# A streaming-encoder layer: elementwise work taken off GpSimd, the first stage rewritten, two inner orders changed

## The chip, the cores and the metric

The kernel runs on one core of a Trainium2 chip. A core has TensorE (PE in the profile, with its weight loads as PEld), VectorE (DVE), ScalarE (ACT), GpSimd (POOL) and SyncE (SP), which here only issues DMAs. The engines run side by side, each its own queue in order, and wait for each other by semaphores. The metric is the device time of one launch in microseconds (us). Before the change the median of three runs is 1245.73 us (1245.38 to 1246.48).

## The reference, cut to what matters

One layer on 1024 tokens with 1024 channels, all float32:

```python
h = rmsnorm(x, norm1_g)                       # per token: x * rsqrt(mean(x^2)+eps) * g
xa, ya, sq, sk, sv, dq, dk, dv = split(h @ w_in)
out_a = rg_lru(causal_dwconv(xa)) * gelu(ya)  # gates by two block matrices, then a scan over time
out_b = stick_breaking(sq, sk, sv)            # 4 heads of 64, strictly causal
out_c = diff_attention(dq, dk, dv)            # softmax(q1 k1) - lam * softmax(q2 k2), 4 heads,
                                              # then an rmsnorm over each head's 64 values (sub-norm)
x = x + concat(out_a, out_b, out_c) @ w_out
u = causal_dwconv(rmsnorm(x, norm2_g) @ w_ff_up)
x = x + (silu(gate(u)) * val(u)) @ w_ff_down
return rmsnorm(x, final_g)
```

## The kernel before, in words

**Split products.** Every large product is made from three products of half operands: an operand is written as `hi` (a cast to a shorter format, fp32r) and `lo` (the rest, operand minus `hi`), and hi·hi, hi·lo and lo·hi are added in PSUM. So each weight tile of 128 x 1024 values costs one cast and one subtraction on an elementwise engine before PE can use it (`split_to`, lines 135 to 152). In the profile a weight is `raw_dk`, `hi_dk`, `lo_dk` and so on, and its product is `pj_dk`. Weight tile number i has its cast on DVE for i below `VECTOR_HI` and its subtraction on GpSimd for i from 4 to 19 (`POOL_LO`), else on DVE.

**First stage** (lines 599 to 625). The 1024 tokens come in eight tiles `x_0` to `x_7`. For each tile a step `n` does the norm: ACT squares and sums the row (`junk`), takes a square root (`ry`); DVE refines 1/sqrt in five small instructions on 128x1 (`rv`, `ry`, `rq`); GpSimd multiplies the row by the gain `gb` (`xg`). The norm factor goes in for tiles 0 to 3 as a diagonal matrix `dg` that PE multiplies with while it transposes, for tiles 4 to 6 by a DVE multiplication, for tile 7 by ACT. A step `t` transposes the tile on PE (`tp`, eight blocks of 128x128), ACT casts the result to `hTh` and DVE subtracts to `hTl`. A step `s` splits weight tiles. The table `START` is the order in which ACT and DVE get these steps; it is kept as written. On PE the order is set by a list scheduler when the program is built, and then stands.

**First projections.** `start_pair` runs `dk` and `dq` on tokens 0 to 511 (24 products each) and then on tokens 512 to 1023; the third weight, `dv`, follows after both. Between the two halves stand `setup_lru` (some thirty DVE instructions on 128x4, `wl`) and `setup_tab` (the distance table `tab`).

**Attention.** A loop over 64 pairs (head, block of 128 queries): scores on PE (`sd`, `ss`), exponentials on ACT, differences or scans on DVE (`e`, `gam`, `bet`). GpSimd masks `gam` and `bet` by a select. The other 17 projections are cut in pieces (`filler`) and handed to PE between these steps. In `weighted` the probabilities of a pair of blocks are transposed chunk by chunk on PE (`pt`), copied by ACT (`ph`), and multiplied with the values (`av`) in `gather`, one chunk behind. `sub_norm` runs once for each pair of heads, one step per loop turn: squares and sums (`sq`, `ssq`), 1/sqrt by small DVE instructions (`bv`, `by`, `bq`), then for each half a broadcast on DVE (`bc`), its transposition on PE (`rb`) and the final product on DVE.

**Rest.** The output projection with the second norm (in its last group, for tokens 512 and up, two sums of the Strassen-like up-projection run on GpSimd: `t4_sum`, `t4_parts`), the gated MLP up-projection, and the down-projection, in which `right_half` multiplies by the final gain on GpSimd.

Instructions emitted through the recording helper all show line L62.

Of the kernel before, what the change touches and what calls it, by code (L numbers as in the profile page):

```python
# [46 lines left out]
def hybrid_trunk(ctx: ExitStack, tc: tile.TileContext, x, norm1_g, w_in, conv_a_w, conv_a_b,  # L47
# [66 lines left out]
    def add_cols(name, w2d, c0):  # L114
        job_no[name] = len(jobs)
        jobs.append((name, w2d[:, c0:c0 + P].rearrange("(k p) c -> p k c", p=P), True, None))
# [52 lines left out]
    for c in range(4):  # L169
# [3 lines left out]
             "xa2", "sk1", "sq1", "sv1", "ya2", "xa3", "ya3"]  # L173
    for nm in first + later:
        add_cols(nm, w_in[0], FT[nm])
# [80 lines left out]
    def transpose_split(xg, dg, hh, hl, t):  # L256
        q = (t % 4) * P
        for j in range(2):
            ps = bank_t(f"tp_{t}_{j}").rearrange("p (a b) -> p a b", a=4)
            for k in range(4):  # L260
                blk = xg[:, (4 * j + k) * P:(4 * j + k + 1) * P]
                if dg is None:
                    T.transpose(out=ps[:, k, :], in_=blk, identity=ident)
                else:
                    T.matmul(ps[:, k, :], lhsT=blk, rhs=dg, start=True, stop=True)
# [22 lines left out]
    wm = bank_t("warm")  # L288
# [54 lines left out]
    def setup_lru():  # L343
# [68 lines left out]
    chores = []  # L412
# [131 lines left out]
    def project(name, early=False):  # L544
        hi, lo = weights(name)
        if early:
            both = two_banks(f"pj_{name}")
        for h in range(2):
            if early:
                ps = both[:, h * HALF:(h + 1) * HALF]  # L550
            else:
                ps = bank_t(f"pj_{name}_{h}")
# [46 lines left out]
    with tc.manual_schedule(engines={nc.scalar.engine, nc.vector.engine}):  # L599
        dg1 = {}  # L600
        for step in START:
            t = int(step[1])
            if step[0] == "n":
                vy = rsqrt_start(xts[t], junk, 1.0 / D)
                xg1[t] = at4(f"xg1_{t}")[:, 0:D]
                cut = D // 4 if t == 0 else 0
                if cut:
                    V.tensor_tensor(xg1[t][:, 0:cut], xts[t][:, 0:cut], gb1[:, 0:cut], ALU.mult)
                G.tensor_tensor(xg1[t][:, cut:D], xts[t][:, cut:D], gb1[:, cut:D], ALU.mult)
                rr = rsqrt_end(*vy)  # L610
                dg1[t] = None
                if SCALE_1[t] == "D":
                    dg1[t] = diagonal(rr, c2(f"dg1_{t}", F32)[:, 0:P])
                elif SCALE_1[t] == "A":
                    A.activation(xg1[t], xg1[t], AF.Identity, scale=rr)
                else:
# [85 lines left out]
    def weighted(ptiles, vt, hh, j, put, name, nh):  # L702
        av = ps1.tile([P, P], F32, tag="av", name=f"av_{name}")
        held = None
# [9 lines left out]
        for c in range(j + 1):  # L714
# [16 lines left out]
        gather(*held)  # L731
# [16 lines left out]
    def sub_norm(p, o):  # L748
        ss = bank_t(f"ssq_{p}")
        for c in range(2):  # L750
            cs = slice(c * HALF, (c + 1) * HALF)
            sq = c2(f"sq_{p}_{c}", F32)
            A.activation(sq, o[:, cs], AF.Square)
            for b in range(4):
                q = 4 * c + b
                T.matmul(ss[:, 2 * q:2 * q + 2], lhsT=sq[:, b * P:(b + 1) * P], rhs=bones,
                         start=True, stop=True)
# [8 lines left out]
        yield  # L766
        for c in range(2):
            cs = slice(c * HALF, (c + 1) * HALF)
            bc_ = c2(f"bc_{p}_{c}", F32)
            V.tensor_copy(bc_.rearrange("p (q h d) -> p q h d", q=4, h=2),  # L770
                          y[:, 8 * c:8 * c + 8].rearrange("p (q h) -> p q h", h=2).unsqueeze(3)
                          .broadcast_to([P, 4, 2, 64]))
            ps = bank_t(f"rb_{p}_{c}")
            for b in range(4):
                T.transpose(out=ps[:, b * P:(b + 1) * P], in_=bc_[:, b * P:(b + 1) * P], identity=ident)
# [568 lines left out]
    for grp in range(4):  # L1344
        toks = (2 * grp, 2 * grp + 1)
        pss = {t: two_banks(f"oc_{t}") for t in toks}
        for ki, kt in enumerate(STREAM + (KEEP if grp == 0 else [])):
# [25 lines left out]
            if grp == 3:  # L1373
                if ki == 1:
# [3 lines left out]
                    t4_sum(4, G)  # L1378
                if ki == 2:
# [4 lines left out]
                    t4_sum(5, G)  # L1384
# [202 lines left out]
    def right_half(t):  # L1587
# [3 lines left out]
        G.tensor_scalar(ssr[t], ssr[t], 1.0 / D, EPS, ALU.mult, ALU.add)  # L1591
        G.tensor_tensor(o, acc[t][:, H1], gfin[:, H1], ALU.mult)
# [113 lines left out]
```

## Time and profile before

| | |
|---|---|
| median of three runs | 1245.73 us |
| profiled execution, its time | 1245.19 us |
| its span, first to last instruction | 1243.5 us |
| PE busy | 1181.2 us (95%) |
| DVE busy | 930.8 us (75%) |
| ACT busy | 638.5 us (51%) |
| GpSimd busy | 137.8 us (11%) |
| mean granted TensorE clock | 0.981 of full |

How to read it: PE is the engine that is nearly always busy, so the time is PE's work, plus PE's idle time, plus what PE loses in stretches in which it was granted less than its full clock. What the other engines do matters where PE waits for them. The rows further down are taken from four views: the page, the waits of PE, the instructions in order of time, and busy time by stretches of the span.

### The profile page before, as it was taken

Reading aid. Unit: us, or ns where it says so; the run is one execution under the profiler, and the core shown is the slowest. Engines: PE = TensorE matmul, PEld = TensorE weight load, DVE = VectorE, ACT = ScalarE, POOL = GpSimd, SP = SyncE. Lnnn points to the kernel's source line nnn. Section 1 sums busy time; section 2 is a strip of 40 time slices with the busy share of each in tenths; the row PEclk is TensorE's granted clock in tenths of the full one; section 3 lists DMA queues with packets and bytes.
Section 4 is the critical chain, followed back from the end, with each engine's and each line's share of the span. In section 5 each row is a group of like instructions: output and inputs, shape, how many; then the busy total and the mean of one; then the engine's idle time right before and its main releaser. Section 6 shows DMA issues by size and latency. Waiting matters only on the chain.

```text
span 1243.5 us, 15374 instructions
## 1 busy us (share of the span) xinstructions
PE 1181.2 (95%) x5731; PEld 918.4 (74%) x5731; DVE 930.8 (75%) x1361; ACT 638.5 (51%) x1046; POOL 137.8 (11%) x187
## 2 busy tenths in 40 slices
PE   5899999999899998998899999999999999999997
PEld 4777676666676666776578888888888888888886
DVE  7746557655763688677999988898888968856776
ACT  3424476637444765543555545545555554433455
POOL 6002011012333230003000000000000000000210
PEclk7989998999899999999999999999999999999999
DMA  5111011201122354831233233332323269832223
GB/s 188 52 34 37 18 35 54 51 22 39 45 52 79 110 169 154 306 102 34 71 100 110 94 110 95 100 111 94 101 90 114 94 207 315 302 107 93 93 77 136
DMA packets 121116, 130.42 MB, mean 105 GB/s; under 512 B 6401, under 2 KB 85713, under 8 KB 121041
## 3 DMA queue, kind: packets, MB, share of 16 engines
q1 hardware_dynamic: 120529, 129.17, 32.5%
q8 instruction: 45, 0.74, 0.2%
q0 software_dynamic: 512, 0.26, 0.1%
q14 instruction: 30, 0.25, 0.1%
HBM read 96.64 MB, written 32.77 MB: 104 GB/s over the span
## 4 chain that ended last, share of the span: by engine, by line
PE 58%; DVE 8%; ACT 4%; issue 3%; DMA 1%; POOL 1%; DVEq 0%; ACTq 0%; POOLq 0%
PE ad L62 18%; PE b L62 10%; PE u L62 9%; PE v L62 7%; PE e L62 4%; PE oc L62 3%; PE av_s L62 1%; PE pj_ya L62 1%; DMA raw_wo<-in_w_out_dram 1%; PE pj_sq L62 1%; PE pj_sv L62 1%; PE pt_s L62 1%; DVE gam L62 1%; PE ss L62 1%; DVE t L62 1%
## 5 line engine op out<-in xcount | busy, mean ns | idle before, releaser
L62 ACT COPY u<-ad 128x512 f32<-128x512 f32 x44 | 25.7, 585 | 116.6 <-PE ad L62 116.6
L62 DVE CUSTOM_DVE_ANT_0 e<-sd,tab 128x128 f32<-128x128 f32 (+7 forms) x64 | 46.3, 754 | 48.1 <-PE sd L62 48.0
L62 ACT ACTIVATE e<-e,mn 128x128 f32<-128x128 f32 (+7 forms) x64 | 49.6, 776 | 51.5 <-DVE mn L62 51.5
L62 DVE TENSOR_TENSOR al<-ar,ah 128x1024 fp32r<-128x1024 f32 x35 | 44.5, 1270 | 42.1 <-ACT ah L62 39.9
L62 ACT CAST ah<-ar 128x1024 fp32r<-128x1024 f32 x35 | 36.6, 1045 | 67.2 <-issue 31.8
L62 PE MATMUL ad<-h2h,xh 128*128 128x512 f32 x176 | 69.8, 397 | 1.1 <-ACT oc L62 1.1
L1591 POOL TENSOR_SCALAR sr<-sr 128x1 f32<-128x1 f32 x8 | 3.5, 432 | 606.8 <-ACT dw L62 606.8
L62 PE MATMUL ad<-h2h,xl 128*128 128x512 f32 x176 | 69.5, 395 | 0.0
L62 PE MATMUL ad<-h2l,xh 128*128 128x512 f32 x176 | 69.5, 395 | 0.0
L62 PE MATMUL e<-T,w 128*128 128x512 f32 x264 | 65.5, 396 | 0.8 <-ACT T L62 0.5
L62 PE MATMUL u<-bh,ah 128*128 128x512 f32 x160 | 62.7, 392 | 0.2 <-DVE cg L62 0.2
L62 PE MATMUL u<-bl,ah 128*128 128x512 f32 x160 | 62.6, 391 | 0.0
L62 PE MATMUL u<-bh,al 128*128 128x512 f32 x160 | 62.5, 391 | 0.0
L62 DVE SCALAR_TENSOR_TENSOR va<-cv,fcol,va 128x1023 f32<-128x1023 f32 (+1 forms) x44 | 56.5, 1284 | 7.0 <-ACT va L62 6.2
L62 DVE TENSOR_TENSOR_SCAN gam<-gam 128x128 f32<-128x128 f32 (+7 forms) x32 | 44.2, 1383 | 22.9 <-POOL gam L679 22.9
L62 PE MATMUL b<-T,yh 128*128 128x512 f32 x176 | 56.6, 403 | 4.2 <-DVE t L62 2.5
L62 DVE SCALAR_TENSOR_TENSOR ga<-cg,fcol,ga 128x1023 f32<-128x1023 f32 (+1 forms) x44 | 56.5, 1283 | 4.8 <-ACT ga L62 3.8
L62 PEld LDWEIGHTS e<-T,w 128*128 128x128 f32 x264 | 49.5, 188 | 13.4 <-ACT T L62 1.0
L62 PE MATMUL b<-B,zh 128*128 128x512 f32 x176 | 55.4, 396 | 1.6 <-DVE cv L62 1.6
L62 PE MATMUL ad<-T,zh 128*128 128x512 f32 x176 | 55.5, 396 | 0.5 <-ACT u L62 0.5
L62 PE MATMUL ad<-T,yh 128*128 128x512 f32 x176 | 55.3, 395 | 0.0
L62 PE MATMUL oc<-hi_wo,mx 128*128 128x512 f32 x160 | 52.7, 399 | 0.4 <-ACT oc L62 0.4
(398 smaller groups left out, 3364.8 us busy)
## 6 DMA issues: line engine op xcount, KB each, us to landing
qd<-g SPq DMA_DIRECT2D x77, 256.0 KB, 2.0
ar<-qd SPq DMA_DIRECT2D x35, 512.0 KB, 4.0
raw_wo<-in_w_out_dram SPq DMA_DIRECT2D x23, 512.0 KB, 3.8
rg<-in_w_ff_up_dram SPq DMA_DIRECT2D x22, 512.0 KB, 5.1
rv<-in_w_ff_up_dram SPq DMA_DIRECT2D x22, 512.0 KB, 4.0
dw<-in_w_ff_down_dram SPq DMA_DIRECT2D x20, 512.0 KB, 6.7
mx<-m SPq DMA_DIRECT2D x24, 256.0 KB, 5.2
x<-in_x_dram SPq DMA_DIRECT2D x8, 512.0 KB, 7.8
```

What stands on the lines that cost most here:

```text
L62: ins = emit(*args, **kw)
L1591: G.tensor_scalar(ssr[t], ssr[t], 1.0 / D, EPS, ALU.mult, ALU.add)
```

## The change

- **First stage.** The norm step is now one DVE instruction over the whole row, `xg = x * r * g`; no diagonal matrices, no GpSimd, no ACT scaling. All eight transpositions use the identity. Four small products of a zero matrix (`warm`) follow the transpositions of tiles 0 to 2. The order table is new: each transposition comes one norm step later, and the first weight is split before the fourth tile's transposition.
- **First weights.** The casts of the first three weights move to ACT. The third weight `dv` gets its own buffer (`third`). `start_three` runs `dk`, `dq` and `dv` on tokens 0 to 511 and then all three on tokens 512 to 1023. `setup` comes between the halves, `setup_tab` later, `setup_lru` becomes a chore taken in four pieces during the attention.
- **GpSimd.** All weight subtractions, `t4_sum`, `t4_parts` and `right_half` go to DVE. GpSimd keeps the fills, the selects, the index table and its 16 small DMAs.
- **Gathers.** `gather` runs for two chunks together, up to two chunks behind.
- **Sub-norm.** Its steps are cut finer: squares; sums; 1/sqrt; both broadcasts; then each half's transposition and product.

```diff
-START = "n0 n1 n2 t0 n3 t1 s1 t2 n4 t3 n5 n6 t4 n7 s2 t5 t6 t7".split()
-SCALE_1 = "DDDDVVVA"
-POOL_LO = range(4, 20)
-VECTOR_HI = 23
+WARM_T = 4
+START = "n0 n1 t0 n2 t1 n3 t2 s1 t3 n4 s2 n5 t4 n6 t5 n7 s3 t6 t7".split()
+VECTOR_HI = range(3, 23)
...
-            if i < VECTOR_HI:
+            if i in VECTOR_HI:
                 V.tensor_copy(hi, raw)
             else:
                 A.copy(hi, raw)
-            (G if i in POOL_LO else V).tensor_tensor(lo, raw, hi, ALU.subtract)
+            V.tensor_tensor(lo, raw, hi, ALU.subtract)
...
+    def start_three(names, between):
+        w = [parts.pop(nm) for nm in names]
+        ps = [two_banks(f"pj_{nm}") for nm in names[:2]]
         for h in range(2):
+            for i, nm in enumerate(names):
+                bank = ps[i][:, h * HALF:(h + 1) * HALF] if i < 2 else bank_t(f"pj_{nm}_{h}")
                 for k in range(KT):
+                    mm3(bank, *w[i], k, h, slice(0, HALF))
+                consumers[nm](h, bank)
+                for fn in between.get((h, i), ()):
                     fn()
...
-                cut = D // 4 if t == 0 else 0
-                if cut:
-                    V.tensor_tensor(xg1[t][:, 0:cut], xts[t][:, 0:cut], gb1[:, 0:cut], ALU.mult)
-                G.tensor_tensor(xg1[t][:, cut:D], xts[t][:, cut:D], gb1[:, cut:D], ALU.mult)
-                rr = rsqrt_end(*vy)
-                dg1[t] = None
-                if SCALE_1[t] == "D":
-                    dg1[t] = diagonal(rr, c2(f"dg1_{t}", F32)[:, 0:P])
-                elif SCALE_1[t] == "A":
-                    A.activation(xg1[t], xg1[t], AF.Identity, scale=rr)
-                else:
-                    V.tensor_scalar(xg1[t], xg1[t], rr, None, ALU.mult)
+                V.scalar_tensor_tensor(xg1[t], xts[t], rsqrt_end(*vy), gb1, ALU.mult, ALU.mult)
             elif step[0] == "t":
-                transpose_split(xg1[t], dg1[t], hTh[t // 4], hTl[t // 4], t)
+                transpose_split(xg1[t], hTh[t // 4], hTl[t // 4], t)
+                if t < 3:
+                    for _ in range(WARM_T):
+                        T.matmul(wm[:, 0:P], lhsT=zero, rhs=xg1[t][:, 0:P], start=True, stop=True)
...
-        setup()
-        start_pair(first[0], first[1], [setup_lru, setup_tab])
-        for _ in project(first[2], early=True):
-            pass
+        load_to(4)
+        start_three(first, {(0, 2): [setup], (1, 0): [lambda: ahead(first[2], 0)], (1, 1): [setup_tab]})
...
-            if held is not None:
-                gather(*held)
-            held = (c, pt)
+            held.append((c, pt))
+            if len(held) == 3:
+                gather(*held.pop(0))
+                gather(*held.pop(0))
...
     def sub_norm(p, o):
+        sqs = [c2(f"sq_{p}_{c}", F32) for c in range(2)]
+        for c in range(2):
+            A.activation(sqs[c], o[:, c * HALF:(c + 1) * HALF], AF.Square)
+        yield
         ss = bank_t(f"ssq_{p}")
...
+        bcs = [c2(f"bc_{p}_{c}", F32) for c in range(2)]
+        for c in range(2):
+            V.tensor_copy(bcs[c].rearrange("p (q h d) -> p q h d", q=4, h=2),
+                          y[:, 8 * c:8 * c + 8].rearrange("p (q h) -> p q h", h=2).unsqueeze(3)
+                          .broadcast_to([P, 4, 2, 64]))
+        yield
...
-                    t4_sum(4, G)
+                    t4_sum(4, V)
...
-                    t4_parts(4, G)
+                    t4_parts(4, V)
                     prep_x(1)
                     prep_x(0)
-                    t4_parts(5, G)
+                    t4_parts(5, V)
...
-        G.tensor_scalar(ssr[t], ssr[t], 1.0 / D, EPS, ALU.mult, ALU.add)
-        G.tensor_tensor(o, acc[t][:, H1], gfin[:, H1], ALU.mult)
+        V.tensor_scalar(ssr[t], ssr[t], 1.0 / D, EPS, ALU.mult, ALU.add)
+        V.tensor_tensor(o, acc[t][:, H1], gfin[:, H1], ALU.mult)
```

How the order moves is shown at three places. First DVE's queue in the opening, from the second norm step to the first tile's `hTl`. Before:

```order
L62 TENSOR_SCALAR dg_1_180<-ident,ry 128x128
L62 TENSOR_SCALAR rv<-ss 128x1
L62 RECIPROCAL ry<-ry 128x1
L62 SCALAR_TENSOR_TENSOR rq<-ry,rv 128x1
L62 TENSOR_SCALAR rq<-rq 128x1
L62 TENSOR_TENSOR ry<-ry,rq 128x1
L62 TENSOR_SCALAR dg_2_195<-ident,ry 128x128
L62 TENSOR_TENSOR hTl_145<-tp_0_197,hTh_143 128x4x128
L62 TENSOR_TENSOR hTl_145<-tp_1_204,hTh_143 128x4x128
```

The same place of DVE's queue in the changed kernel:

```order
L61 SCALAR_TENSOR_TENSOR xg_1_170<-x_1_125,ry,gb_121 128x1024
L61 TENSOR_TENSOR hTl_145<-tp_0_177,hTh_143 128x4x128
L61 TENSOR_TENSOR hTl_145<-tp_1_184,hTh_143 128x4x128
L61 TENSOR_SCALAR rv<-ss 128x1
L61 RECIPROCAL ry<-ry 128x1
L61 SCALAR_TENSOR_TENSOR rq<-ry,rv 128x1
L61 TENSOR_SCALAR rq<-rq 128x1
L61 TENSOR_TENSOR ry<-ry,rq 128x1
L61 SCALAR_TENSOR_TENSOR xg_2_201<-x_2_127,ry,gb_121 128x1024
```

The first tile's subtraction moved ahead of the third norm, and the wide multiplication stands in DVE's queue.

Second PE's queue at the seams between the first products: end of `dq` on the first tokens, start of `dk` on the last tokens, and the seam from `dq` to `dv`. Before:

```order
L62 MATMUL pj_dq_413<-hTh_143,lo_dq_343 128x512
L62 MATMUL pj_dk_412<-hTh_144,hi_dk_240 128x512
...
L62 MATMUL pj_dq_413<-hTh_144,lo_dq_343 128x512
L62 MATMUL pj_dv_559<-hTh_143,hi_dv_467 128x512
L62 MATMUL pj_dv_559<-hTl_145,hi_dv_467 128x512
```

PE's queue at the same seams in the changed kernel:

```order
L61 MATMUL pj_dq_395<-hTh_143,lo_dq_289 128x512
L61 MATMUL tp_1_385<-ident,xg_7_352 128x128 x4
L61 MATMUL pj_dv_0_449<-hTh_143,third 128x512
L61 MATMUL pj_dv_0_449<-hTl_145,third 128x512
...
L61 MATMUL pj_dv_0_449<-hTh_143,third 128x512
L61 MATMUL pj_dk_394<-hTh_144,hi_dk_257 128x512
```

`dv` on the first tokens moved ahead of `dk` on the last tokens, and the last transposition stands just before it.

Third PE's queue at the sub-norm of the first head pair, where `rb` transposes the first broadcast `bc_0`. Before:

```order
L62 MATMUL sd_6_0_1914<-qk_d_715 128x384
L62 MATMUL sd_6_1_1915<-qk_d_715 128x384
L62 MATMUL rb_0_1869<-ident,bc_0_1867 128x128 x4
L62 MATMUL pt_d_1_1_1878<-ident,e_3_0_1725 128x128
L62 MATMUL pt_d_1_1_1878<-ident,e_2_0_1651 128x128
```

PE's queue around the same transposition in the changed kernel:

```order
L61 MATMUL pt_d_2_0_1981<-ident,e_5_0_1844 128x128
L61 MATMUL sd_7_0_2001<-qk_d_700 128x512
L61 MATMUL sd_7_1_2002<-qk_d_700 128x512
L61 MATMUL rb_0_2018<-ident,bc_0_1918 128x128 x4
L61 MATMUL pj_sq_0_2024<-hTh_143,hi_sq_1822 128x512
```

`rb_0` moved back by more than one loop turn: from behind the scores of block 6 to behind those of block 7.

## Rows read from the trace of the kernel before

**Rows 1.** The page: busy time, share of the span and instructions of each engine.

```profile
PE 1181.2 (95%) x5731; PEld 918.4 (74%) x5731; DVE 930.8 (75%) x1361; ACT 638.5 (51%) x1046; POOL 137.8 (11%) x187
```

**Rows 2.** By stretch: us, length, each engine's busy us, granted clock, DMA share, GB/s.

```profile
0.00:31.00 31.00, 15.71 (x84) 14.77 (x84) 23.33 (x33) 11.95 (x24) 20.69 (x25) 0.78 0.55 189
...
124.00:400.00 276.00, 263.26 (x1542) 189.22 (x1542) 167.33 (x308) 151.82 (x288) 58.33 (x85) 0.96 0.15 43
```

**Rows 3.** PE's waits: what waited for what: us in total, times, longest us.

```profile
PE tp L62 <- DVE rv L62: 7.4, 1, 7.4
PE rb L62 <- DVE bc L62: 5.9, 2, 3.9
PE pj_dv L62 <- DVE qk_d L62: 4.0, 1, 4.0
...
PE av_d L62 <- ACT ph_d L62: 2.1, 1, 2.1
PE av_s L62 <- ACT ph_s L62: 1.8, 1, 1.8
```

**Rows 4.** DVE in order of time: start us, us, operation; 20 to 62 us.

```profile
20.53 2.12 DVE L62 SCALAR_TENSOR_TENSOR rq<-ry,rv 128x1 f32<-128x1 f32 x1
...
23.27 1.28 DVE L62 TENSOR_TENSOR hTl<-tp,hTh 128x512 fp32r<-128x512 f32 x2
24.47 0.14 DVE L62 TENSOR_SCALAR rv<-ss 128x1 f32<-128x1 f32 x1
...
24.72 0.22 DVE L62 SCALAR_TENSOR_TENSOR rq<-ry,rv 128x1 f32<-128x1 f32 x1
...
25.36 0.29 DVE L62 TENSOR_SCALAR dg<-ident,ry 128x128 f32<-128x128 f32 x1
...
29.16 1.23 DVE L62 TENSOR_TENSOR lo_dk<-raw_dk,hi_dk 128x1024 fp32r<-128x1024 f32 x1
...
61.65 1.23 DVE L62 SCALAR_TENSOR_TENSOR tab<-tab 128x1024 f32<-128x1024 f32 x1
```

**Rows 5.** GpSimd in order of time, first stage.

```profile
6.73 15.90 POOL L609 TENSOR_TENSOR xg<-x,gb 128x768 f32<-128x768 f32 x7 [4.50 <-DMA gb<-in_norm_g_dram]
```

**Rows 6.** By stretch, at 18 to 22 us, columns as in the second group.

```profile
18.00:22.00 4.00, 1.23 (x8) 0.97 (x8) 3.93 (x4) 1.46 (x4) 4.00 (x2) 0.93 0.12 28
```

**Rows 7.** ACT in order of time, the second tile's norm.

```profile
7.89 1.06 ACT L62 ACTIVATE junk<-x 128x1024 f32<-128x1024 f32 x1 [1.91 <-DMA x<-in_x_dram]
...
9.07 0.29 ACT L62 ACTIVATE ry<-ss,eps 128x1 f32<-128x1 f32 x1
```

**Rows 8.** PE in order of time, first projections, with idle time ahead in brackets.

```profile
33.37 1.16 PE L62 MATMUL tp<-ident,xg 128*128 128x128 f32 x8 [0.92 <-DVE xg L62]
34.28 0.48 PE L62 MATMUL pj_dk<-hTl,hi_dk 128*128 128x512 f32 x1
...
63.53 0.79 PE L62 MATMUL pj_dv<-hTh,hi_dv 128*128 128x512 f32 x1 [4.00 <-DVE qk_d L62]
...
79.80 0.48 PE L62 MATMUL pj_dk<-hTh,hi_dk 128*128 128x512 f32 x1
```

**Rows 9.** By stretch, three stretches at a low granted clock.

```profile
63.50:69.00 5.50, 5.46 (x13) 4.30 (x14) 2.46 (x3) 0.00 (x0) 0.00 (x0) 0.50 0.31 88
...
204.00:212.00 8.00, 8.00 (x27) 6.73 (x27) 6.62 (x17) 1.89 (x5) 0.00 (x0) 0.50 0.20 59
...
332.00:336.00 4.00, 4.00 (x13) 3.12 (x12) 1.69 (x3) 1.37 (x2) 0.00 (x0) 0.57 0.00 0
```

**Rows 10.** Groups by line: DVE at 60 to 485 us, and GpSimd.

```profile
L62 DVE SCALAR_TENSOR_TENSOR s<-s,nlam,s 128x1 f32<-128x1 f32 x32 | 14.4, 450 | 1.0
...
L150 POOL TENSOR_TENSOR lo_ya<-raw_ya,hi_ya 128x1024 fp32r<-128x1024 f32 x4 | 9.6, 2392 | 50.5 <-DVE hi_ya L62 40.1 <-PE pj_ya L62 7.8 <-PE pt_s L62 2.6
...
L1592 POOL TENSOR_TENSOR dw<-acc03b,gfin 128x512 f32<-128x512 f32 x4 | 7.4, 1844 | 0.3
```

**Rows 11.** DVE in order of time, end of the output projection.

```profile
570.71 2.31 DVE L62 TENSOR_TENSOR xl<-rg,xh 128x1024 fp32r<-128x1024 f32 x1
```

More of the change, by code (lines that the diff above doesn't have):

```diff
@@ L112, in hybrid_trunk, with add_cols @@
     direct = set()
-    def add_cols(name, w2d, c0):
+    def add_cols(name, w2d, c0, dst=None):
         job_no[name] = len(jobs)
-        jobs.append((name, w2d[:, c0:c0 + P].rearrange("(k p) c -> p k c", p=P), True, None))
+        jobs.append((name, w2d[:, c0:c0 + P].rearrange("(k p) c -> p k c", p=P), True, dst))
     def add_row(name, w2d, k, dst=None):
@@ L173, in hybrid_trunk, with third @@
              "xa2", "sk1", "sq1", "sv1", "ya2", "xa3", "ya3"]
+    def third():
+        w = b16("third", (P, 2, 8, P))
+        return w[:, 0], w[:, 1]
     for nm in first + later:
-        add_cols(nm, w_in[0], FT[nm])
+        add_cols(nm, w_in[0], FT[nm], third if nm == first[2] else None)
     STREAM = [6, 0, 1, 7, 4]
@@ L253, in rsqrt_bits, with transpose_split @@
         return y
-    def transpose_split(xg, dg, hh, hl, t):
+    def transpose_split(xg, hh, hl, t):
         q = (t % 4) * P
@@ L260, in transpose_split @@
             for k in range(4):
-                blk = xg[:, (4 * j + k) * P:(4 * j + k + 1) * P]
-                if dg is None:
-                    T.transpose(out=ps[:, k, :], in_=blk, identity=ident)
-                else:
-                    T.matmul(ps[:, k, :], lhsT=blk, rhs=dg, start=True, stop=True)
+                T.transpose(out=ps[:, k, :], in_=xg[:, (4 * j + k) * P:(4 * j + k + 1) * P], identity=ident)
             h = hh[:, 4 * j:4 * j + 4, q:q + P]
@@ L285, in c2 @@
         return att.tile([P, HALF], dt, tag="c2", name=name, bufs=6)
-    wm = bank_t("warm")
+    wm = ps1.tile([P, P], F32, tag="av", name="warm")
     for _ in range(WARM):
@@ L358, in setup_lru @@
             V.tensor_scalar(po, po, 1.0 / n, None, ALU.add)
+            if n in (9, 3):
+                yield
         V.tensor_tensor(po, po, z, ALU.mult)
@@ L411, in hybrid_trunk @@
     lru = {}
-    chores = []
+    chores = [setup_lru()]
     last_scan = []
@@ L541, in hybrid_trunk, with project @@
         consumers[f"ya{c}"] = branch_y(c)
-    def project(name, early=False):
+    def project(name):
         hi, lo = weights(name)
-        if early:
-            both = two_banks(f"pj_{name}")
         for h in range(2):
[L549 to L552, printed above, removed]
+            ps = bank_t(f"pj_{name}_{h}")
             for k in range(KT):
@@ L599, in hybrid_trunk @@
     with tc.manual_schedule(engines={nc.scalar.engine, nc.vector.engine}):
-        dg1 = {}
         for step in START:
@@ L703, in weighted @@
         av = ps1.tile([P, P], F32, tag="av", name=f"av_{name}")
-        held = None
+        held = []
         def gather(c, pt):
@@ L725, in weighted @@
                 V.tensor_copy(pt[:, b0 * P:], tp[:, b0 * P:])
-            if held is not None:
-                gather(*held)
-            held = (c, pt)
+            held.append((c, pt))
+            if len(held) == 3:
+                gather(*held.pop(0))
+                gather(*held.pop(0))
             yield
         yield
-        gather(*held)
+        for h_ in held:
+            gather(*h_)
         put(av)
@@ L748, in sub_norm @@
     def sub_norm(p, o):
+        sqs = [c2(f"sq_{p}_{c}", F32) for c in range(2)]
+        for c in range(2):
+            A.activation(sqs[c], o[:, c * HALF:(c + 1) * HALF], AF.Square)
+        yield
         ss = bank_t(f"ssq_{p}")
[L750 to L757, printed above, removed]
+        for q in range(8):
+            T.matmul(ss[:, 2 * q:2 * q + 2], lhsT=sqs[q // 4][:, (q % 4) * P:(q % 4 + 1) * P], rhs=bones,
+                     start=True, stop=True)
         c1 = sums[p]
@@ L766, in sub_norm @@
         yield
+        bcs = [c2(f"bc_{p}_{c}", F32) for c in range(2)]
[3 more added lines that the diff above has]
+                          .broadcast_to([P, 4, 2, 64]))
+        yield
         for c in range(2):
             cs = slice(c * HALF, (c + 1) * HALF)
[L769 to L772, printed above, removed]
             ps = bank_t(f"rb_{p}_{c}")
             for b in range(4):
-                T.transpose(out=ps[:, b * P:(b + 1) * P], in_=bc_[:, b * P:(b + 1) * P], identity=ident)
+                T.transpose(out=ps[:, b * P:(b + 1) * P], in_=bcs[c][:, b * P:(b + 1) * P], identity=ident)
             V.scalar_tensor_tensor(o[:, cs], o[:, cs], gsub, ps, ALU.mult, ALU.mult)
@@ L968, in norm2_t @@
             B["h"], B["l"] = b16("h2h"), b16("h2l")
-        transpose_split(hns.pop(t), None, B["h"], B["l"], t)
+        transpose_split(hns.pop(t), B["h"], B["l"], t)
     def banks_of(t):
@@ L1383, in hybrid_trunk @@
                     last_tokens(5)
-                    t4_sum(5, G)
+                    t4_sum(5, V)
                 if ki == 4:
-                    t4_parts(4, G)
+                    t4_parts(4, V)
                     prep_x(1)
                     prep_x(0)
-                    t4_parts(5, G)
+                    t4_parts(5, V)
         if grp == 0:
```

13 lines of the change are left out of this document (removed).

## The prediction

> **What bounds the kernel now.** I read the page's busy times first. PE works 95% of the span [rows 1], so the time is PE's work plus what PE idles or loses to a low clock. Then the stretches: in the first 31 us PE is busy for 15.7 us at a mean granted clock of 0.78, and from 124 to 400 us it idles 276.0 - 263.3 = 12.7 us at 0.96, while DVE is busy 167 of 276 us, 61% [rows 2]. Third, PE's waits name the places: the first transpositions, the sub-norm's `rb`, the start of `dv`, and the value products `av` that wait for their copied chunks [rows 3]. Only these places can give time back; a DVE or GpSimd instruction elsewhere costs nothing.
>
> The opening is slow for a reason that the order of instructions shows. An instruction on 128x1 values (`rq`) takes 2.12 us at 20.5 us and 0.22 us four microseconds later [rows 4]. In between GpSimd ends its seven gain products, 15.9 us in one go from 6.7 us on [rows 5]. It isn't the DMA traffic: at 18 to 22 us the DMA engines are busy for 0.12 of the time, and DVE is still full [rows 6]. So DVE's small instructions wait for GpSimd's, and every norm step pays several of these 2 us.
>
> **First stage.** The change empties GpSimd there and prices everything on DVE by undisturbed rows. A norm chain takes 25.36 - 24.47 = 0.9 us [rows 4]. The wide `xg`, two SBUF operands and a scalar on 128x1024, isn't in the trace; the nearest row is `tab`, the same operation and size, 1.23 us, 1.2 back to back. A tile's two `hTl` are 24.47 - 23.27 = 1.2, a weight's `lo` 1.2 [rows 4]. The second tile's square root ends at 9.07 + 0.29 = 9.4 us, and the tile itself had landed at 7.9 [rows 7]. From there DVE has, before PE can run the first product without a stop: three norm steps (3 x 2.1), the `hTl` of three tiles (3 x 1.2), `lo_dk` (1.2) and half the fourth tile's `hTl` (0.6). That is 11.7, so PE starts at 9.4 + 11.7 = 21.1 us, where it now starts at 34.3 [rows 8]. ACT's casts and squares run beside it.
>
> From there to the first product of the next weight (`dk1`) PE now takes 79.8 - 34.3 = 45.5 us [rows 8]. Of this go the wait of 4.0 before `dv` [rows 3, 8], since thirty `wl` instructions and the table no longer stand in front of `qk_d`, and half of the 5.5 us at clock 0.50 behind that wait, 2.7 [rows 9]. One tile's transpositions come in, 1.2 [rows 8]. That leaves 40.0, and `dk1` starts at 61.1: 18.7 us earlier.
>
> Does DVE keep up with three first halves? After 21.1 it has half an `hTl`, four norm steps, four `hTl` and two `lo`: 0.6 + 8.4 + 4.8 + 2.4 = 16.2, done at 37.3. PE's 72 products take about 0.21 us each at full clock (13 take 5.5 us at half [rows 9]), 15.1, and four tiles' transpositions 4.6, so it needs the second tokens at 40.8. The margin is 3.5 us; at `dv`, whose `lo` comes at about 34.5, it is about 1 us. SP now puts three weight loads ahead of the nine small parameter loads; the third waits for a buffer until `dv` is split, so these come 20 us later than now, and their transposition on PE stands some 10 us behind that. I price this at nothing; if they are late, PE stands still for the difference. I take 18 of the 18.7. The bounds are 4 (only the `dv` wait goes) and 20.
>
> The clock is the weak point. PE has some 2.4 us of work in each 3.3 us step from 8 to 19 us, with gaps. If the clock falls there, the first products run at half speed, as the thirteen at 63.5 us do, at a price of 2.7 us [rows 9]. The Trainium skill, "TensorE: Matmul & The Clock Gate", section "Part 4: PE-mode transpose", says that transpositions do not count as PE activity for the clock. By that rule only the twelve small `warm` products would hold the clock, and the gain would be 15 to 16 us; no run here shows yet which holds.
>
> **Attention, PE's waits.** `rb` waits 5.9 us in two places [rows 3], and after each the clock is low: 8.0 us at 0.50 and 4.0 us at 0.57 cost 4.0 + 1.7 = 5.7 us [rows 9]. In the new order a loop turn lies between the broadcast and `rb`, so the wait has cover. The `av` waits are 2.1 + 1.8 = 3.9 [rows 3]; gathering up to two chunks later gives the copies more time. The sum of all is 15.5. Two thirds of it, 10, is what I take: PE's order is fixed anew, and some waits will come up where there were none. Bounds are -3 and 16.
>
> **Attention, DVE's load.** Sixteen weight subtractions come from GpSimd, where one takes 2.39 us [rows 10], to DVE at 1.23 [rows 4]: 19.7 us. Against this DVE loses fewer waits: the 32 small `s` products alone have a mean of 0.45 us where 0.22 is undisturbed, 7.4 us together [rows 4, 10]. Net 12 us at most over more than 300 us, with DVE at 61%. PE's filler covers it: nothing. Without cover each subtraction costs PE its 1.23.
>
> **End of the output projection and tail.** `t4_sum` and `t4_parts` are six half-width DVE instructions, 0.6 to 0.7 each by the `hTl` row, 4 us; a neighbour that takes 2.31 us now, beside GpSimd, should take 1.2 [rows 4, 11], and two more like it. Net 1, and I take 0.5. In the tail eight half-width products and eight tiny ones come to DVE, about 0.8 each, 6.4 us; DVE also waits there now for ACT's square. GpSimd took 1.84 for one [rows 10]. PE doesn't wait in that stretch, so I take 0.5, with 0 to 4 as bounds.
>
> **Sum.** -18 - 10 + 1 = -27. The profiled execution took 1245.19 us (span 1243.5 and 1.7 around it), so 1218.2; the median of the runs lies 0.5 higher, which gives 1218.7, rounded 1218.5.
>
> **The rivals.**
> 1. *The opening alone.* The waits in the attention move elsewhere, since DVE still runs the same chains in a fixed order and is a little fuller. For: PE lost only 12.7 us there [rows 2]. Against: the two `rb` waits have a plain cause. 1245.7 - 18 + 1 = 1228.7.
> 2. *The clock is low at the first products* (the rule above, worked as the thirteen slow products): 2.7 us dearer, 1221.
> 3. *The change doesn't do what it says:* the 2 us instructions aren't GpSimd's doing but come from the crowded DMA queues, which carry the same loads. Then only the 4.0 before `dv` goes: about 1241. Against it is the stretch at 18 to 22 us [rows 6].
> 4. *Slower: DVE becomes the bound of the attention.* The place is DVE's queue at 60 to 400 us: each subtraction stands in front of a score reduction or a probability that PE waits for. Sixteen times 1.23 is 19.7 [rows 4]; four of these stops also pull the clock down, at 1.7 to 4.0 each [rows 9], 11; nothing of the 10 comes back. 1245.7 - 18 + 31 + 1 = 1260. It outweighs the opening from the point at which PE idles 31 us instead of 12.7 between 124 and 400. Against it stands DVE at 61% [rows 2]. The Trainium skill, "Perfetto Trace Analysis", section "Optimizing Scalar/DVE Operations", says that moving work to ACT or GpSimd may make sense when DVE is saturated, and this change goes the other way; at 61% the trace doesn't show a saturated DVE.
>
> **How the numbers follow.** Forecast 0.58; rival 1, 0.23; rival 2, 0.08; rival 3, 0.06; rival 4, 0.05. The forecast's own range is 1209 to 1226, from the bounds of the two large terms taken half way. The range for 8 in 10 takes in rivals 1 and 2 and reaches below for an attention that gives all 16 and an opening that gives 20: 1206 to 1235. A measurement of this kernel tells 0.2% from no change, 2.5 us. Faster by more: the forecast, rivals 1 and 2, and half of 3: 0.92. Within: 0.03. Slower: rival 4, 0.05.
>
> **What would show it.** In the changed profile: `rq` at 0.2 us in every norm step; the first `pj_dk` products back to back from about 21 us and `dk1` from about 61; no wait before `dv`; the granted clock full from 20 us on; no `rb` wait over 1 us and fewer than 8 us of PE idle in the attention up to where the scores end; DVE busier by about 10 us in all. It would be wrong if `rq` stays at 2 us, if `pj_dv` waits for `third` or `pt` for its loads by more than 3 us, or if new PE waits for DVE's `lo`, `e` or `bet` add up to more than 10 us.

## The result and the profile after

The changed kernel takes 1209.97 us (median, 1206.47 to 1211.89), the kernel before took 1246.11 beside it: a ratio of 0.9704 with a 95% interval of 0.9677 to 0.9731, or 36 us less. Forecast were 1218.5, within 1206 to 1235. The profiled execution has a span of 1207.2 us.

First the page of the kernel after, with each engine's busy us and share, then stretches (us, length, busy us of PE, PEld, DVE, ACT and GpSimd, granted clock, DMA share, GB/s).

```profile
PE 1163.9 (96%) x5723; PEld 906.9 (75%) x5723; DVE 928.1 (77%) x1396; ACT 639.6 (53%) x1048; POOL 55.8 (5%) x141
```

```profile
0.00:31.00 31.00, 23.37 (x138) 20.05 (x139) 23.07 (x56) 21.71 (x41) 2.49 (x17) 1.00 0.66 221
...
124.00:400.00 276.00, 268.93 (x1595) 195.19 (x1595) 183.04 (x320) 168.12 (x310) 40.17 (x100) 0.99 0.20 55
```

Beside [rows 1, 2]: PE does 7.7 us more in the first 31 us, and the clock there is 1.00 instead of 0.78. GpSimd gave up 82 us of work, and yet DVE, which took most of it over, is 2.7 us *less* busy. DVE in the first stage shows why (start us, us, operation):

```profile
16.14 0.22 DVE L61 SCALAR_TENSOR_TENSOR rq<-ry,rv 128x1 f32<-128x1 f32 x1
...
16.78 1.28 DVE L61 SCALAR_TENSOR_TENSOR xg<-x,ry,gb 128x1024 f32<-128x1024 f32 x1
17.98 1.28 DVE L61 TENSOR_TENSOR hTl<-tp,hTh 128x512 fp32r<-128x512 f32 x2
19.18 1.21 DVE L61 TENSOR_TENSOR lo_dk<-raw_dk,hi_dk 128x1024 fp32r<-128x1024 f32 x1
```

`rq` takes 0.22 us, not 2.12 [rows 4]. The other part of the answer, from the attention, is in experiment 6. PE in order of time:

```profile
21.05 0.50 PE L61 MATMUL pj_dk<-hTl,hi_dk 128*128 128x512 f32 x1 [1.04 <-DVE hTl L61]
...
35.87 0.50 PE L61 MATMUL pj_dv<-hTh,third 128*128 128x512 f32 x1
...
59.90 0.48 PE L61 MATMUL pj_dk<-hTh,hi_dk 128*128 128x512 f32 x1
```

The last wait of the opening ends at 21.05, `dv` starts without one, and `dk1` starts at 59.90 instead of 79.80 [rows 8]. PE's waits that are left (us in total, times, longest):

```profile
PE tp L61 <- DVE xg L61: 7.5, 6, 1.6
PE pt_s L61 <- DVE bet L61: 4.2, 3, 1.9
...
PE av_s L61 <- DVE ph_s L61: 0.9, 1, 0.9
```

Of [rows 3], `tp<-rv`, `rb<-bc` and `pj_dv` are gone, `av_d` and `av_s` for ACT as good as gone.

Where the 36 us come from is read at three marks that both programs pass: the last product of `dk1`, the first and last of the `hi_wo` products, the first `ad` (ns min/median/max, first to last start in us). Before, then after:

```profile
L62 PE MATMUL pj_dk<-hTh,lo_dk x32: 387/389/478, 34.6 to 93.8; 128*128 128x512 f32 x32
...
L62 PE MATMUL oc<-hi_wo,mx x160: 387/393/500, 463.9 to 566.2; 128*128 128x512 f32 x160
...
L62 PE MATMUL ad<-h2h,xh x176: 389/393/500, 575.9 to 1008.8; 128*128 128x512 f32 x176
```

```profile
L61 PE MATMUL pj_dk<-hTh,lo_dk x32: 387/389/476, 21.4 to 73.9; 128*128 128x512 f32 x32
...
L61 PE MATMUL oc<-hi_wo,mx x160: 387/392/501, 425.4 to 530.0; 128*128 128x512 f32 x160
...
L61 PE MATMUL ad<-h2h,xh x176: 389/394/476, 538.5 to 972.6; 128*128 128x512 f32 x176
```

Up to the last `dk1` product 19.9 us are gained (93.8 to 73.9). From there to the first `hi_wo` product, called the attention from here on, 370.1 becomes 351.5: 18.6. The output projection takes 113.1 instead of 112.0, and the rest 668.7 instead of 667.6: 2.2 given back. That is the span's 36.3.

Summing PE's idle time and (1 - clock) over slices of 4 us splits the attention further: idle 15.5 before and 8.4 after, lost to the clock 10.2 and 3.4, and what remains 344.4 and 339.7. So 7.1 + 6.8 came from waits and the clock behind them, and 4.7 from somewhere else: PE's busy time itself.

### The profile page after: what moved, and what is told of

The parts are those of the page before. It is cut to its first block, busy times and chain, and to the rows that moved or that the text cites. A ratio compares the mean times of both kernels' runs of the same rounds, so it can differ in the third digit from the quotient of the medians.

```text
span 1207.2 us, 15321 instructions
## 1 busy us (share of the span) xinstructions
PE 1163.9 (96%) x5723; PEld 906.9 (75%) x5723; DVE 928.1 (77%) x1396; ACT 639.6 (53%) x1048; POOL 55.8 (5%) x141
## 4 chain that ended last, share of the span: by engine, by line
PE 77%; DVE 11%; ACT 6%; issue 3%; DMA 1%; POOL 1%; SPq 0%; DVEq 0%; POOLq 0%; ACTq 0%
PE ad L61 18%; PE b L61 10%; PE u L61 9%; PE v L61 8%; PE e L61 5%; PE pj_ya L61 3%; PE sd L61 2%; PE oc L61 2%; PE pj_sq L61 2%; PE pj_dq L61 2%; PE pj_dk L61 2%; PE pj_sv L61 2%; PE pj_xa L61 2%; PE pj_dv L61 2%; PE av_d L61 1%
## 5 line engine op out<-in xcount | busy, mean ns | idle before, releaser
L61 DVE TENSOR_TENSOR al<-ar,ah 128x1024 fp32r<-128x1024 f32 x35 | 42.8, 1223 | 37.1 <-ACT ah L61 34.9
L61 PEld LDWEIGHTS e<-T,w 128*128 128x128 f32 x264 | 49.3, 187 | 13.1 <-DVE T L61 0.5
L61 DVE TENSOR_TENSOR_SCAN gam<-gam 128x128 f32<-128x128 f32 (+7 forms) x32 | 44.4, 1389 | 15.5 <-POOL gam L661 15.4
L61 PE MATMUL v<-bl,ah 128*128 128x512 f32 x120 | 46.9, 391 | 0.0
```

Of the source, the lines that this page charges most:

```text
L61: ins = emit(*args, **kw)
```

## The experiments

All are edits of the changed kernel; its own time is taken as 1210. Ratios are to the kernel before, with 95% intervals. "The attention" is the stretch between the two marks above, 351.5 us in the changed kernel and in every variant that doesn't touch it (351.5, 351.6, 351.5).

**1. GpSimd busy beside the first stage.**

```
+ for h in range(2):          # t = 1 to 7; nothing reads it
+     G.tensor_tensor(beside, xts[t][half h], gb1[half h], ALU.mult)
```

> The changed kernel, with fourteen 128x512 products of tokens and gain given to GpSimd beside the norm steps; nothing reads their results. Theory (GpSimd's SBUF traffic stretches DVE's small instructions): `rq` is back at about 2 us while they run, DVE ends its eleven microseconds of work later, the first `pj_dk` product comes at about 29 us (27 to 33) instead of 21.05, and the time rises by 5 to 11 us. Rival (the long `rq` came from the DMA queues, and the new order made the gain): `rq` stays at 0.2 us and the time stays within 1 us.

1221.02 us, 0.9788 (0.9768 to 0.9808): 11 us slower, at the upper end. The first product without a stop comes at 30.37 us. DVE in that kernel, in order of time, then the group of GpSimd (busy us, mean ns):

```profile
15.54 0.14 DVE L61 TENSOR_SCALAR rv<-ss 128x1 f32<-128x1 f32 x1
...
15.79 1.01 DVE L61 SCALAR_TENSOR_TENSOR rq<-ry,rv 128x1 f32<-128x1 f32 x1
16.84 0.15 DVE L61 TENSOR_SCALAR rq<-rq 128x1 f32<-128x1 f32 x1
17.03 1.01 DVE L61 TENSOR_TENSOR ry<-ry,rq 128x1 f32<-128x1 f32 x1
18.07 2.25 DVE L61 SCALAR_TENSOR_TENSOR xg<-x,ry,gb 128x1024 f32<-128x1024 f32 x1
20.25 1.28 DVE L61 TENSOR_TENSOR hTl<-tp,hTh 128x512 fp32r<-128x512 f32 x2
```

```profile
L600 POOL TENSOR_TENSOR beside<-x,gb 128x512 f32<-128x512 f32 x14 | 20.3, 1490 | 6.1 <-DMA x<-in_x_dram 6.1
```

Theory and rival part cleanly: the DMA loads are the same, and `rq` is long again, though 1.01 us and not the 2 expected. Not every instruction stretches: those with two tensors in SBUF do (0.22 to 1.01, 1.28 to 2.25), the 128x1 ones with one (0.15) and `hTl`, which reads one of its two from PSUM (0.64 each), do not. But the count of tensors alone doesn't decide it. In the kernel before, `dg`, with one tensor and a 128x1 factor, took 2.33 us beside GpSimd, where 0.29 is undisturbed [rows 4]:

```profile
18.03 2.33 DVE L62 TENSOR_SCALAR dg<-ident,ry 128x128 f32<-128x128 f32 x1
```

And the wait goes with the length of GpSimd's instruction: 1.01 beside 512 columns, 2.12 beside 1024. The `rq` of [rows 4] ends at 20.53 + 2.12 = 22.65 us, and GpSimd's last product at 6.73 + 15.90 = 22.63 [rows 5]. The Trainium skill, "SBUF — State Buffer", section "Who interferes with whom", says that a DVE instruction with two SBUF inputs contends with a GpSimd instruction that reads SBUF, that one with at most one SBUF input does not unless it runs in a mode that uses both ports, and that DMA never contends with a compute engine. These rows agree with the first, and with the third: in the changed kernel `rq` takes 0.22 at 16.14 us, where the DMA share is 1.07 (14 to 18 us). On the second they agree for the 128x1 instructions and `hTl`; in which mode `dg` ran no run here shows.

**2. No small products behind the transpositions.**

```
- WARM_T = 4
+ WARM_T = 0
```

> The changed kernel without the twelve `warm` products behind the first three tiles' transpositions. Theory A (transpositions don't hold the clock, the small products do): the granted clock falls below 0.7 between 10 and 22 us, the first `pj_dk` products run at half speed for some 5 us, and the time rises by 2 to 4 us. Theory B (the transpositions alone hold it, or the clock in this stretch is a toss-up in either kernel): the clock at 18 to 26 us lies between 0.64 and 1.00, as in the runs with the `warm` products, and the time stays within 1 us.

1210.76 us, 0.9708 (0.9691 to 0.9725). Stretches, with the clock third from the end:

```profile
10.00:14.00 4.00, 1.97 (x8) 1.57 (x8) 3.79 (x11) 2.68 (x6) 0.00 (x0) 0.56 1.09 378
14.00:18.00 4.00, 1.94 (x8) 1.57 (x8) 3.86 (x9) 3.17 (x7) 0.98 (x1) 0.50 1.07 362
18.00:22.00 4.00, 3.42 (x11) 2.63 (x12) 3.74 (x7) 2.80 (x6) 0.01 (x1) 0.50 0.07 21
```

Theory A has the clock right, and its price is too high for this run. The clock is 0.50 where PE runs transpositions only, and 1.00 there in the changed kernel with the small products between them. The rule weighed in the prediction (the Trainium skill, "TensorE: Matmul & The Clock Gate", "Part 4: PE-mode transpose") fits that. But `dv` starts at 36.9 instead of 35.9: 1.0 us, not 2 to 4. Up to 21 us PE waits for DVE in any case, and from 25 us on the clock is 1.00 again, so that only the first products run slowly. With the small products the clock isn't safe either. Five other runs of the same opening (experiments 4, 5, 7, 10 and 12) show 0.64 to 0.93 between 18 and 26 us, and `dv` starts at 36.8 to 37.1 in them, so that the small products' worth can't be told from that. In a sixth, experiment 3, the clock was lower for longer, and `dv` started at 38.5, 2.6 us late:

```profile
22.00:26.00 4.00, 4.00 (x11) 3.14 (x10) 3.75 (x11) 1.89 (x4) 0.00 (x0) 0.50 0.42 123
26.00:31.00 5.00, 5.00 (x29) 4.21 (x28) 3.35 (x9) 2.62 (x6) 0.00 (x0) 0.86 0.37 110
```

**3. The opening alone**: sub-norm, gather, the sixteen `lo` and the end's four helpers as before (the edits of experiments 4 to 7 together).

> The opening of the changed kernel alone: sub-norm, gather, the sixteen subtractions and the end's GpSimd work as before. Theory (the opening gives the 20 us by which the first `dk1` product came earlier, and keeps them): 1226 us (1223 to 1229), and the attention's waits before `rb`, `av_d` and `av_s` are those of the kernel before. Rival (the parts need each other: the attention of before is what the new opening runs into): under 1221 or over 1231.

1229.53 us, 0.9860 (0.9836 to 0.9884): 17 us faster than before, 19 slower than with the rest, and half a microsecond above the theory's range. In its trace the last `dk1` product starts at 76.5, 17.3 us earlier than before; the 2.6 that are missing from 19.9 are the clock's (experiment 2). The attention takes 372.9 us, 2.8 more than before, with `rb` 5.9, `av_d` 2.1 and `av_s` 1.8 of waits, to the tenth those of [rows 3]. So the two halves are about equal, and the opening keeps its gain with the old attention. The new attention behind the old opening was not run.

**4. The sub-norm in its old steps.**

```
- sqs ...; yield; ssq ...; yield; rsqrt_bits ...; yield; bcs ...; yield; rb ...
+ sq, ssq ...; yield; rsqrt_bits ...; yield; bc_, rb ... (in one step)
```

> The changed kernel with the sub-norm in its three old steps. Theory (the waits before `rb` and the low clock behind them are what the eight steps remove): `rb<-bc` waits 5 to 6 us again, the clock is at 0.5 behind two of the waits, and the time rises by 9 to 12 us. Rival (the idle time only moves to another product): 2 us or less.

1222.52 us, 0.9808 (0.9790 to 0.9826): 12.5 slower, a little more than expected; the attention is 13.1 longer: 3.7 more idle, 10.2 more lost to the clock, 0.8 less of the rest. But `rb` waits only once, and the longest stretch at a low clock lies 120 us ahead of it, behind a wait before `av_d`. Both waits in order of time, then the clock behind each:

```profile
180.83 0.72 PE L61 MATMUL av_d<-ph_d,v_dv 128*64 128x128 f32 x6 [2.11 <-ACT ph_d L61]
...
311.95 1.12 PE L61 MATMUL rb<-ident,bc 128*128 128x128 f32 x4 [2.79 <-DVE bc L61]
```

```profile
180.00:184.00 4.00, 3.17 (x16) 2.84 (x17) 3.35 (x7) 3.52 (x8) 0.00 (x0) 0.66 0.63 200
184.00:188.00 4.00, 4.00 (x14) 3.48 (x14) 1.62 (x5) 0.30 (x2) 0.00 (x0) 0.50 0.04 8
188.00:192.00 4.00, 4.00 (x14) 3.16 (x13) 3.52 (x8) 0.59 (x1) 0.00 (x0) 0.56 0.00 0
...
312.00:316.00 4.00, 4.00 (x12) 3.29 (x13) 2.18 (x4) 1.02 (x2) 0.00 (x0) 0.50 0.00 0
316.00:320.00 4.00, 4.00 (x18) 3.21 (x17) 1.16 (x2) 2.92 (x6) 0.63 (x1) 0.77 0.00 0
```

PE is fully busy from 184 to 192 and gets 14 products done in 4 us; 24 to 33 are usual here. A third low stretch, from about 202 to 209, follows two waits of 0.8 and 0.9 us before `sd`. So the theory is right on the sum and on the kind of loss, and wrong on the place: the wait before `rb` and the clock behind it make some 6 of the 13 us. The rest comes from waits before `av_d` and `sd`. In the changed kernel three products of `pj_sk` stand between `sd` and `av_d` there, and `av_d` waits 0.5. Why PE's order came out so wasn't tested. Of this term the low clock is about three quarters, the idle time the rest.

**5. One chunk gathered at a time.**

```
- held.append((c, pt)); if len(held) == 3: gather two
+ if held is not None: gather(*held)
+ held = (c, pt)
```

> The changed kernel with the value products of one chunk at a time again. Theory (a later gather gives the copies time): `av` waits 3 to 4 us again and the time rises by 2 to 4 us. Rival (PE waits the same time elsewhere): within 1 us.

1217.92 us, 0.9773 (0.9753 to 0.9794): 8 us, twice the theory's most, and for another reason. PE from 60 to 420 us in the kernel after, in this one, and in experiment 8:

```profile
60.00:420.00 360.00, 352.36 (x2107) 256.32 (x2106) 241.54 (x460) 212.62 (x410) 48.80 (x116) 0.99 0.21 60
```

```profile
60.00:420.00 360.00, 352.31 (x2042) 251.16 (x2041) 232.07 (x454) 203.97 (x393) 44.31 (x107) 0.99 0.19 54
```

```profile
60.00:420.00 360.00, 352.06 (x2143) 259.83 (x2141) 245.56 (x463) 217.53 (x416) 53.56 (x122) 0.99 0.21 61
```

The same busy time at the same clock, and 65 products fewer, respectively 36 more. The waits hardly changed. Of the 9.8 us by which the attention grew, idle time gives -0.4, the clock 1.7 and busy time 8.5. What differs is how often PE goes from one sort of product to another: in its order `av` stands in 78 stretches here, in 56 in the changed kernel and in 77 before; `pt` in 81, 77 and 81; the projections in 152 each time. The chunk's three transpositions, first this kernel, then the one after:

```profile
250.16 0.49 PE L61 MATMUL pt_d<-ident,e 128*128 128x128 f32 x3
250.58 0.66 PE L61 MATMUL av_d<-ph_d,v_dv 128*64 128x128 f32 x8
251.17 0.50 PE L61 MATMUL pj_sv<-hTh,hi_sv 128*128 128x512 f32 x1
251.50 0.39 PE L61 MATMUL pj_sv<-hTl,hi_sv 128*128 128x512 f32 x1
```

```profile
244.28 0.39 PE L61 MATMUL pj_sv<-hTh,lo_sv 128*128 128x512 f32 x1
244.51 0.49 PE L61 MATMUL pt_d<-ident,e 128*128 128x128 f32 x3
244.75 0.47 PE L61 MATMUL pj_sv<-hTh,hi_sv 128*128 128x512 f32 x1
```

Ahead of a projection three transpositions take 0.24 us (244.51 to 244.75), ahead of `av` 0.42; the first projection product behind a small group takes 0.33 to the next start (251.17 to 251.50), where 0.23 is usual. Over the whole attention of these two traces, from start to start, the last `pt` of a group is followed by `av` after 0.20 to 0.21 us on average and by a projection after 0.03; the last `av` is followed by a projection after 0.21, by another `av` after 0.06. So a stretch of `av` more costs about 0.3 us, and 22 of them make 7 of the 8.5. It is booked as busy. What PE does in that time the traces don't show.

**6. The sixteen `lo` on GpSimd.**

```
- V.tensor_tensor(lo, raw, hi, ALU.subtract)
+ (G if i in range(4, 20) else V).tensor_tensor(lo, raw, hi, ALU.subtract)
```

> The changed kernel, with the `lo` subtractions of sixteen weights (4 to 19) on GpSimd again and nothing else undone. Theory (contention): DVE loses 16 x 1.2 = 19 us of work and gets nearly all of it back as stretched small instructions, so that it is busy for 925 us or more and PE's waits grow; slower by 3 to 8 us. Rival (the gain of the attention is the sub-norm's and the gather's alone): DVE is some 15 us less busy, the time is the same or up to 2 us shorter.

1212.28 us, 0.9724 (0.9707 to 0.9740): 2.3 slower by the medians; the intervals overlap, the attention is 2.3 longer too. DVE's and GpSimd's groups (count, busy us, mean ns):

```profile
L61 DVE SCALAR_TENSOR_TENSOR s<-s,nlam,s 128x1 f32<-128x1 f32 x32 | 10.4, 326 | 0.9
...
L149 POOL TENSOR_TENSOR lo_ya<-raw_ya,hi_ya 128x1024 fp32r<-128x1024 f32 x4 | 9.6, 2393 | 49.2 <-DVE hi_ya L61 38.4 <-PE pj_ya L61 8.2 <-PE pt_s L61 2.6
```

In the kernel after the same two are

```profile
L61 DVE SCALAR_TENSOR_TENSOR s<-s,nlam,s 128x1 f32<-128x1 f32 x32 | 7.0, 219 | 0.9
...
L61 DVE TENSOR_TENSOR lo_ya<-raw_ya,hi_ya 128x1024 fp32r<-128x1024 f32 x4 | 4.9, 1221 | 0.3
```

Sixteen times 1.22 us leave DVE, 19.5, and its busy time falls by 7.7 only (928.1 to 920.4): 60% comes back as stretched instructions. The `s` are 3.4 of it, `e` on 384 and `bet` on 896 columns 4.0 together. The sign is the theory's, the size below its range.

**7. The end's helpers on GpSimd.**

```
- t4_sum(4, V) ... V.tensor_scalar(ssr[t], ...); V.tensor_tensor(o, acc[t][:, H1], gfin[:, H1], ALU.mult)
+ t4_sum(4, G) ... G.tensor_scalar(ssr[t], ...); G.tensor_tensor(o, acc[t][:, H1], gfin[:, H1], ALU.mult)
```

> The changed kernel with `t4_sum`, `t4_parts` and the two instructions of `right_half` on GpSimd again. Theory (their move to DVE is worth little either way, and the 2 us that the output projection gives back have another cause): the time stays within 2 us of the changed kernel's. Rival (DVE is full from 425 us on, and the moved work is what the end of the output projection gives back): 2 to 4 us faster than the changed kernel, the first `ad` product about 2 us earlier against the first `oc`.

1208.33 us, 0.9692 (0.9670 to 0.9713): within the 2 us. Its trace has the output projection at 111.5 instead of 113.1 and the rest at 668.0 instead of 668.7. But other variants that leave the helpers on DVE (experiments 1, 2, 4, 5, 6, 9 and 12) have the output projection at 112.5 to 115.1, so that no comparison here tells a cost of the move from none.

**8. All chunks of an output together.**

```
- if len(held) == 3:
-     gather(*held.pop(0))
-     gather(*held.pop(0))
```

> The changed kernel with all chunks of an output gathered together, at its end, instead of two at a time. Theory (what the gather of two saves is not waits for copies, but stretches of PE: each small group between 512-column products costs PE at its start and behind it, and `av` has 56 stretches where one chunk at a time has 77 to 78): about 32 to 40 stretches and 3 to 8 us faster than the changed kernel. Rival (it saved the waits for the copies, and these are gone): within 1.5 us of the changed kernel. A third way: the chunks hold their buffers for longer, the copies wait for buffers, and it is slower by 2 us or more.

1205.42 us, 0.9671 (0.9647 to 0.9696): 39 stretches of `av`, 4.6 us faster by the medians; the intervals overlap. The attention is 5.6 shorter. Hardly a wait is taken away (idle 7.9 after 8.4); busy time falls by another 5.1, 17 stretches at 0.3. The output projection gives part of it back, with 116.3 us instead of 113.1. The longest wait in it, in this kernel:

```profile
PE oc L61 <- ACT oc L61: 2.7, 1, 2.7
```

**9. Projections six products at a time** between the attention's pieces.

```
- fill_to(int(quota + QUOTA[n] * (at + 1) / len(sched)))
+ fill_to(int(quota + QUOTA[n] * (at + 1) / len(sched)) // 2 * 2)
```

> The changed kernel with the projections' products put between the attention's pieces six at a time instead of three (the same number in all): 129 stretches of them instead of 152 in PE's order, with the stretches of `av`, `pt` and `sd` as they are. Theory (each change of PE from one sort of product to another costs, whichever sort): 23 stretches fewer at the 0.3 to 0.4 us that the gather's stretches cost, so 4 to 8 us faster than the changed kernel. Rival (only the gather's stretches cost, because `av` waits for a copy at the start of each): within 1.5 us. A third way (the projections came in time to cover waits, and now come too late): slower by 2 us or more, with new idle time of PE before `pt` or `av`.

1205.25 us, 0.9671 (0.9650 to 0.9693). The sign and size are the theory's by the median; the attention is shorter by 2.4 only, the rest of the 4.7 lies in stretches that the edit doesn't touch. And the 2.4 are not the theory's sort of gain: 1.8 is idle time, 0.6 busy time. PE from 60 to 420 us, beside 352.36 in the changed kernel (experiment 5):

```profile
60.00:420.00 360.00, 354.10 (x2129) 0.99 0.21 61
```

PE idles 1.7 us less and does 22 products more. So a price for each change, whichever sort, isn't borne out; what experiments 5 and 8 show is a price of the stretches of `av`. Why PE idles less here wasn't settled.

**10 and 11. The versions that might be best**: experiments 7 and 8 together, then 9 with them.

> All chunks gathered together and the end's four helpers on GpSimd, as a version that may beat the changed kernel. If the two are independent and the second is worth what one comparison gave it: 1203.8 us (1202 to 1206), 6 us faster than the changed kernel. If the second is nothing: 1205.4, the time of the gather alone.

> The same with the projections' products six at a time too: 128 stretches of them, 40 of `av`. If every stretch costs and the waits have cover: 1198 us (1195 to 1201). If the projections come too late to cover the copies: slower than the same kernel with three at a time, over 1205.

1205.90 (0.9675, 0.9652 to 0.9697) and 1204.69 (0.9664, 0.9643 to 0.9685). The first confirms that the helpers are worth nothing that can be measured. The second is the fastest of all, but misses its 1198 by far: its attention is 7.6 shorter, nearly as the sum wants (5.6 and 2.4), and its output projection takes 116.5 instead of 113.1. PE stands still for 2.6 us there, for ACT's `oc`, at 454 us, and the clock falls behind it (3.4 us). The same wait and the same length, 116.3 and 116.2, stand in experiments 8 and 10, so they come with gathering all chunks and not with the six products. What ACT waited for wasn't settled. Against the changed kernel the gain of 5 to 6 us is likely, though the intervals still touch.

**12. The changed kernel again.**

> The changed kernel itself once more, since every difference above is taken from its median of 1210.0 us, which came from four runs. If that median is good, 1208.5 to 1211.5 us and the gather of all chunks is 3 to 6 us faster. If it was high by chance, 1206 to 1208, and the gather of all chunks is not shown to be faster. The granted clock between 18 and 26 us may lie at 0.6 to 0.9, as in some of the runs with the same opening, which then costs about 1 us.

1210.49 us, 0.9712 (0.9688 to 0.9737): the base holds.

## Why the prediction was right, and where it was wrong

*First stage, 18 (of 18.7) forecast.* Right in mechanism and size: 19.9 at the mark, 17 by experiment 3. GpSimd's part in it is shown by experiment 1, which takes 11 us back; that the other part comes from the order of the three weights is read from the wait before `dv` that is gone, and no run undoes that order alone. The first product without a stop was forecast for 21.1 and came at 21.05, `dk1` for 61.1 and came at 59.9. The durations were read from undisturbed rows, and all came back: `lo_dk` 1.21, `hTl` 0.64, and `xg` 1.28 where 1.2 from `tab` was taken. Three edits that were costed at nothing were hidden: the later small parameter loads made no wait, `dv` found its weights, and DVE kept up.

*The clock (rival 2).* Its mechanism is real (experiment 2): PE had only 2.0 to 2.4 us of work in 4 us between 10 and 18 us, less than the prediction counted on. Its price of 2.7 us came up once (2.6, in experiment 3's trace); where the clock recovers sooner, it is about 1. That the profiled run of the changed kernel had the full clock there is luck, since the same opening shows both.

*Rival 3,* DMA instead of GpSimd, is refuted by experiment 1.

*Attention waits, 10 of 15.5.* This is the step that failed, by size, and in part by a misreading. The misreading: of the two stretches at a low clock that were put behind `rb` [rows 9], only the second is. PE of the kernel before:

```profile
201.67 0.66 PE L62 MATMUL av_d<-ph_d,v_dv 128*64 128x128 f32 x6 [2.09 <-ACT ph_d L62]
...
221.19 0.66 PE L62 MATMUL rb<-ident,bc 128*128 128x128 f32 x4 [2.02 <-DVE bc L62]
...
331.15 1.12 PE L62 MATMUL rb<-ident,bc 128*128 128x128 f32 x4 [3.90 <-DVE bc L62]
```

The stretch at 204 to 212 us follows the wait before `av_d`, and the first `rb` comes 9 us after it. So 4.0 of the 5.7 us of clock belong to the waits before `av_d` and `ssq` (0.8 at 203.1), for which the loop turn put before `rb` gives no cover; the total of 15.5 holds them all the same. As to the size, the attention gave 18.6. Two things are in the difference. First, the factor of two thirds: idle time and clock gave 13.9 of the 15.5, because hardly a new wait came up (idle 8.4 in all, against "fewer than 8"). Second, a term that the sum didn't have: PE's busy time, 4.7 of the 18.6. The sum priced the gather by the waits before `av`, 3.9, and experiment 5 shows 8 to 10 against the changed kernel, nearly all of it busy time of PE. The list of waits can't show it. The single steps (13.1, 9.8 and 2.3 in the attention) add up to 25.2 and give 21.4 together, so they share some of it.

*DVE's load, 0 forecast, "busier by about 10 us".* Wrong in sign: DVE is 2.7 us less busy, and moving the sixteen `lo` is itself worth some 2 us. The prediction counted what the 32 `s` would give back (7.4, as measured: 14.4 before [rows 10], 7.0 after), but not the other instructions with two operands in SBUF. Experiment 6 shows them. Rival 4, a DVE that bounds the attention, has nothing for it.

*End and tail, +1.* The trace has +2.2, and experiment 7 is 2.3 faster in its trace's two stretches; with 112.5 to 115.1 for the output projection in the variants that is too small to tell. `xl` beside it takes 1.22 instead of 2.31 [rows 11], as forecast.

*Rival 1, 1228.7,* is what experiment 3 measured for the opening alone (1229.5). It fell as a forecast because the waits did not move elsewhere. That the median came so close to 1228.7 is in part chance: its trace has a slower opening and a longer attention than the rival counted on.

## What to carry to other kernels

An engine that is off the critical path can still set the pace: look for the same small instruction at two durations in the trace, and for what runs on GpSimd beside the long one. When work moves between the two, price the instructions that get shorter as well as those that move. On a PE that is nearly full, count the stretches of small products as well as the waits, since what a stretch of `av` costs here (0.3 us) is booked as busy time. And before a low clock is put down to a wait, find the wait that stands just ahead of it in order of time.

## What the runs showed that was not expected

- Equal busy time of PE isn't equal work: 2042, 2107 and 2143 products in 352 us at the same clock, by nothing but their grouping.
- A `rq` of 128x1 lasts 0.22 us alone, 1.01 beside 512-column and 2.12 beside 1024-column instructions of GpSimd: it seems to wait for the one that runs to end (22.65 and 22.63 us).
- After 2.1 us of idle time before `av_d` the clock stays at half for about 10 us, after 2.8 before `rb` for about 7 (experiment 4), so the stall costs more behind it than in it.
- In the opening the clock differs from run to run with the same instructions (1.00 or 0.5 to 0.9 at 18 to 26 us), worth about 1 us, once 2.6.
